# Weight pieces in one list of thirteen places, or in separate pools for raw pieces, block sums and split pieces

## The chip, the cores and the metric

One Trainium2 chip, one of its cores. The metric is the device time of the whole program in microseconds (us); lower is better. Before the change three runs gave a median of 2485.02 us (2480.92 to 2485.55).

## The reference

A two-layer decoder trunk over 256 tokens of width 2048, all in float32. Each layer adds a normed mixer and then a normed SwiGLU feed-forward network (5632 hidden columns) to its input:

```python
for layer in range(DEPTH):
    u = rms_norm(h, mix_norm_pre[layer])
    u = even_mixer(u, ...) if layer % 2 == 0 else odd_mixer(u, ...)
    h = h + rms_norm(u, mix_norm_post[layer])
    u = swiglu(rms_norm(h, ffn_norm_pre[layer]), ffn_w_gate[layer], ffn_w_up[layer], ffn_w_down[layer])
    h = h + rms_norm(u, ffn_norm_post[layer])
```

The even mixer is stick-breaking attention beside a gated delta rule, the odd one block-sparse attention beside dilated attention; each has one projection of the input ahead of it and one of the output behind it. Nearly all arithmetic is the product of 256 tokens with the weights (about 400 MB, each read once).

## The kernel before

**Pieces.** The weights are cut on the host into pieces of 128 partitions x 2 x 512 columns, 512 KB, which is 4 KB in each partition. `Builder.run` lines them up in one list of steps, 808 in all: even input projection, even output projection, feed-forward, then the same for the odd layer. Each phase runs in `run_phase`.

**A plain piece** is loaded by SP (L247) and then split for exact products in TensorE's fp32r format: ACT copies it rounded (L222, the high part), DVE subtracts that from the raw values (L223, the low part). In feed-forward phases one operation on each engine does the whole piece (128x1024), elsewhere two of 128x512. TensorE then makes 12 matmuls of 512 columns (`step`, L280 to L282: two halves of the piece, high x high, high x low, low x high, for two blocks of 128 tokens). The high and the low part lie in one tile of 8 KB per partition.

**A seven-product piece** (the last three steps of a `FastChunk`, which is every up chunk of the feed-forward network and every gate chunk but the first) uses a Strassen-like scheme: DVE forms four block sums (L266 on 512 columns, L267 and L268 on 256), the seven blocks of 256 columns are split by one ACT and one DVE operation (128x1792), and TensorE makes 21 matmuls of 256 columns (`fast_step`, L304 to L306) in the place of 24 matmuls' worth of products. Its split parts need two places of 8 KB. There are 42 such chunks, so 126 such pieces; a chunk is five plain pieces and then three seven-product pieces.

**The order of feed-forward chunks.** The 11 column groups are taken in pairs: up, gate, up and gate chunks follow each other, then four down chunks of the pair before (16 plain pieces), and so on.

**The places.** All of this lies in one list of 13 places of 8 KB, `self.wp`, handed out first in, first out, by the program that writes the instructions. A raw plain piece takes half a place (`self.half`, shared with the next one). A raw seven-product piece takes a whole one, its lower half the weights, its upper half the four sums. `load_until(n)` writes the instructions that load and split piece after piece ahead of step n. It stops at ten steps ahead, or when too few places are free:

```python
need = s.places + (not held or s.pair is not None)
if len(self.wp.free) < need + (self.spare - 1 - held if self.loaded > n else 0):
    break
```

`self.spare` is 5 in feed-forward phases: with no half open, a plain piece is taken up when 6 of the 13 places are free, a seven-product piece when 7 are. Each of the 13 places is a tile with a tag of its own, so a transfer or a split waits for the last reader of just the place that it was given.

**What sets the order on the engines.** The program above fixes the data flow and a priority; a scheduler places the instructions on the five queues by its own estimate of when each could run. All queues run in order on the chip.

Of the kernel before, what the change touches and what calls it, by code (L numbers as in the profile page):

```python
# [28 lines left out]
F32 = mybir.dt.float32  # L29
F32R = mybir.dt.float32r  # L30
# [5 lines left out]
P = 128  # L36
# [6 lines left out]
EPS = 1e-6  # L43
NEG = -1.0e30
WB = 10
WPLACES = 13
SPARE = 3
SPARE_FFN = 5
LAG_FFN = 1
DEFER = 5  # L50
LAG = 4
# [13 lines left out]
class Step:  # L65
# [3 lines left out]
    def __init__(self, src, kts, chunk, first, last, pair=None):  # L69
        self.src, self.kts, self.chunk, self.first, self.last, self.pair = src, kts, chunk, first, last, pair  # L70
        self.wh = self.wl = None
        self.ends = last
        self.places = 1 if pair is None else 2
# [73 lines left out]
class Builder:  # L147
    def __init__(self, tc, I, out, pool):
        self.tc, self.nc, self.I, self.out = tc, tc.nc, I, out
        self.const = pool("const", bufs=1)  # L150
        wpool = pool("w", bufs=1)
        self.tmp = pool("tmp", bufs=1)
        big = pool("big", bufs=1)
        psb = pool("psb", bufs=1, space=PSUM)
        dram = pool("dram", bufs=1, space=bass.MemoryType.DRAM)
        self.mem = Pool(big, "m", NTILES)
        self.wp = Pool(wpool, "w", WPLACES, (P, 2048))
        self.spare, self.lag, self.half = SPARE, LAG, None
        self.ps = Pool(psb, "p", NPS)
        self.pa = Pool(psb, "acc", PSA)  # L160
        self.cin = Pool(big, "c", 2, (P, 4, P + 3))
        self.xd = dram.tile([2 * P, D], F32, name="xd", tag="xd")
        self.nwd = dram.tile([4, D], F32, name="nwd", tag="nwd")
        self.work, self.steps, self.flags, self.loaded = [], [], set(), 0
        self.unsplit = [set(), set()]
        self.S = None
        self.x, self.y, self.yss, self.aT, self.r = ([None] * 2 for _ in range(5))
        self.mix = [{}, {}]
# [60 lines left out]
    def load_until(self, n, end=None):  # L229

        nc = self.nc
        while self.loaded < min(n + WB if end is None else end, len(self.steps)):
            s = self.steps[self.loaded]
            held = self.half is not None
            need = s.places + (not held or s.pair is not None)
            if len(self.wp.free) < need + (self.spare - 1 - held if self.loaded > n else 0):
                break
            s.w = [self.wp.pop(1) for i in range(s.places)]
            w = [a.bitcast(F32R) for a in s.w]
            if s.pair is None:  # L240
                n_ = s.src.shape[2]
                done = self.half
                self.half = done or self.wp.pop(1)
                raw = self.half[:, 1024:] if done else self.half[:, :1024]
                raw, s.wh, s.wl = (a.rearrange("p (k n) -> p k n", k=2)[:, :, :n_]
                                   for a in (raw, w[0][:, :1024], w[0][:, 1024:]))
                nc.sync.dma_start(out=raw, in_=s.src)  # L247
                if s.chunk.ffn:
                    self.split(s.wh, s.wl, raw)
                else:  # L250
                    for j in range(2):
                        self.split(s.wh[:, j], s.wl[:, j], raw[:, j])
                if done:
                    self.half = None
            else:
                done = self.wp.pop(1)
                nc.sync.dma_start(out=done[:, :1024], in_=s.src.rearrange("p k n -> p (k n)"))
                self.split_sums(done.rearrange("p (b n) -> p b n", b=8), s, *w)
            if done:
                self.wp.give(done)  # L260
            self.loaded += 1

    def split_sums(self, b, s, wh, wl):

        nc = self.nc
        nc.vector.tensor_sub(b[:, 4:6], b[:, 0:1].broadcast_to([P, 2, 256]), b[:, 1:3])  # L266
        nc.vector.tensor_sub(b[:, 6], b[:, 1], b[:, 5])  # L267
        nc.vector.tensor_sub(b[:, 7], b[:, 3], b[:, 6])  # L268
        s.wh, s.wl = (a.rearrange("p (b n) -> p b n", b=8)[:, :7] for a in (wh, wl))
        self.split(s.wh, s.wl, b[:, 1:8])  # L270

    def step(self, t, s):
        nc, ch = self.nc, s.chunk
# [63 lines left out]
    def run_phase(self, lo, hi, end):  # L337

        n0 = n1 = lo
        while n1 < hi:  # L340
            edge = n0 - lo < LAG_EDGE or hi - n0 <= LAG_EDGE - self.lag
            lag = LAG_EDGE if edge else max(self.lag, LAG_EDGE - (n0 - lo - LAG_EDGE) // 2)
            if n0 < hi and self.steps[n0].pair is not None:
                if n0 == n1:
                    self.fast_step(self.steps[n0])
                    self.wp.give(*self.steps[n1].w)
                    n0 += 1
                    n1 += 1
                    self.load_until(n1)
                    continue  # L350
                lag = 0
            if n0 < hi and n0 - n1 < lag:
                self.step(0, self.steps[n0])
                n0 += 1
                if n0 == hi:
                    end(0)
            else:
                self.step(1, self.steps[n1])
                self.wp.give(*self.steps[n1].w)
                n1 += 1  # L360
                self.load_until(n1)
        end(1)
# [134 lines left out]
    def run(self):  # L497
        nc, I = self.nc, self.I
        phases = [self.plan_even_in(), self.plan_out(0), self.plan_ffn(0),
                  self.plan_odd_in(), self.plan_out(1), self.plan_ffn(1)]  # L500
        ends = [lambda t: self.end_in(t, 0), lambda t: self.end_out(t, 0), lambda t: self.end_ffn(t, 0),
                lambda t: self.end_in(t, 1), lambda t: self.end_out(t, 1), lambda t: self.end_ffn(t, 1)]
        bounds = []
        for chunks in phases:
            lo = len(self.steps)
            for c in chunks:
                self.steps += c.steps
            bounds.append((lo, len(self.steps)))
        nc.scalar.preload_act_table_set("natural_log_exp_and_others")
        self.ident = self.ld("ident", [P, P])  # L510
        self.nw = self.ld("nw", [P, 4 * KT])
        self.zero = self.fill("zero", [P, P], 0.0)
        self.mhalf = self.fill("mhalf", [P, 8], -0.5)
        self.warm_up()
        self.aT = [[], []]
        self.x = [self.now(self.mem, 4) for t in range(2)]
        for c in range(4):
            for t in range(2):
                self.load_x(t, c, I["x"], nc.sync)
            self.load_until(0, 2 * c + 2)  # L520
        for c in range(4):
            for t in range(2):
                self.first_transposed(t, c)
        for t in range(2):
            self.prenorm_factor(t)
            self.mem.give(*self.x[t])
        self.load_until(0)
        self.load_constants()
        for i, ((lo, hi), end) in enumerate(zip(bounds, ends)):
            if i % 3 == 2:  # L530
                for j in range(PS_FFN):
                    self.ps.lend(self.pa)
                if i == 2:
                    self.mem.give(*self.lev)
                else:
                    self.mem.give(self.mask)
                self.spare, self.lag = SPARE_FFN, LAG_FFN
            self.run_phase(lo, hi, end)
            self.spare, self.lag = SPARE, LAG
            if i % 3 == 2:  # L540
                for j in range(PS_FFN):
                    self.pa.lend(self.ps)
# [798 lines left out]
```

## Time and profile before

| | |
|---|---|
| runs | 2485.02 us median of 3 |
| the profiled execution | 2482.63 us, of which the span of the program's instructions is 2480.9 us |
| TensorE matmul (PE) busy | 2395.2 us, 97% |
| DVE busy | 1752.4 us, 71% |
| ACT busy | 1222.8 us, 49% |
| DMA | 453.67 MB, mean 183 GB/s over the span |
| mean granted TensorE clock | 0.985 |

A row of the profile gives an engine, a source line and the tiles written and read. Matmuls are pipelined, so one that is shown as 0.39 us long is followed by the next after 0.23 us; a gap in the rows is shorter than the time lost. The clock of TensorE is given as a share of its full rate: 1.00 is 2.4 GHz, 0.5 is 1.2 GHz. The feed-forward network of the first layer runs from about 545 to 1300 us, that of the second from about 1710 us to the end.

### The profile page before, as it was taken

What the parts mean: (1) busy time and instruction counts of PE and PEld (TensorE: products, weight loads), DVE (VectorE), ACT (ScalarE), POOL (GpSimd) and SP (SyncE); (2) the same over time, 40 slices, a digit from 0 to 9 for tenths busy, and PEclk for the clock granted to TensorE, in tenths of its full rate; (3) what the DMA queues carried; (4) which work ended last, traced back from release to release, by engine and by line L of the source; (5) the groups of instructions that cost most, each with busy time, mean ns of one, the idle gap of its engine ahead of it and who ended that gap; (6) DMA issues with size and microseconds to landing.
All of it is one profiled execution on the core that took longest, in us unless ns stands there. A gap on an engine that the chain in (4) does not pass through costs nothing.

```text
span 2480.9 us, 32443 instructions
## 1 busy us (share of the span) xinstructions
PE 2395.2 (97%) x12235; PEld 2005.1 (81%) x12235; DVE 1752.4 (71%) x2669; ACT 1222.8 (49%) x1833; POOL 206.2 (8%) x265
## 2 busy tenths in 40 slices
PE   9999999899999999999999999999999999999998
PEld 7878877778888887888877888887878888888876
DVE  7865775577868787778776555566776868687775
ACT  6654563454545444445455544454454535444443
POOL 0330360200000000000121000101000000000011
PEclk9999999999999999999999999999999999999999
DMA  6533434454545645555575444554464645555563
GB/s 235 196 136 136 153 136 149 152 192 163 199 165 187 212 162 197 185 212 178 204 259 186 160 168 181 206 205 166 158 229 161 215 156 204 186 186 180 189 245 126
DMA packets 131133, 453.67 MB, mean 183 GB/s; under 512 B 15568, under 2 KB 20944, under 8 KB 130976
## 3 DMA queue, kind: packets, MB, share of 16 engines
q1 hardware_dynamic: 120704, 423.81, 48.5%
q0 software_dynamic: 8112, 26.52, 3.3%
q8 instruction: 96, 1.57, 0.3%
q10 hardware_dynamic: 2160, 1.27, 0.2%
q14 instruction: 61, 0.50, 0.1%
HBM read 443.11 MB, written 8.42 MB: 182 GB/s over the span
## 4 chain that ended last, share of the span: by engine, by line
PE 65%; DVE 8%; DMA 8%; ACT 3%; issue 2%; POOL 0%; SPq 0%; DVEq 0%; POOLq 0%; ACTq 0%
PE acc L280 9%; PE p L281 9%; PE p L282 9%; PE p L280 9%; PE acc L281 9%; PE acc L282 9%; DVE w L223 4%; DMA w<-in_ffn_w_gate 4%; DMA w<-in_ffn_w_up 3%; ACT w L222 2%; PE acc L305 1%; PE acc L306 1%; PE p L305 1%; PE acc L304 1%; PE p L306 1%
## 5 line engine op out<-in xcount | busy, mean ns | idle before, releaser
L223 DVE TENSOR_TENSOR w<-w,w 128x512 fp32r<-128x512 f32 (+3 forms) x1104 | 1112.7, 1040 | 482.1 <-ACT w L222 479.7
L222 ACT ACTIVATE w<-w 128x512 fp32r<-128x512 f32 (+3 forms) x1104 | 944.4, 892 | 929.0 <-DVE w L268 287.6
L280 PE MATMUL acc<-w,m 128*128 128x512 f32 (+2 forms) x1582 | 622.3, 396 | 16.3 <-ACT w L222 9.0
L281 PE MATMUL acc<-w,m 128*128 128x512 f32 (+2 forms) x1582 | 622.0, 394 | 0.0
L282 PE MATMUL acc<-w,m 128*128 128x512 f32 (+2 forms) x1582 | 621.5, 394 | 0.2 <-DVE m L226 0.2
L280 PE MATMUL p<-w,m 128*128 128x512 f32 x1146 | 454.2, 399 | 10.7 <-ACT w L222 8.7
L281 PE MATMUL p<-w,m 128*128 128x512 f32 x1146 | 455.3, 397 | 0.9 <-DVE w L223 0.8
L282 PE MATMUL p<-w,m 128*128 128x512 f32 x1146 | 454.9, 398 | 0.0
L280 PEld LDWEIGHTS acc<-w,m 128*128 128x128 f32 x1582 | 299.5, 190 | 82.5 <-ACT w L222 10.2
L282 PEld LDWEIGHTS acc<-w,m 128*128 128x128 f32 x1582 | 298.8, 189 | 66.6 <-DVE m L226 0.6
L281 PEld LDWEIGHTS acc<-w,m 128*128 128x128 f32 x1582 | 299.0, 189 | 65.6 <-DVE w L223 0.6
L280 PEld LDWEIGHTS p<-w,m 128*128 128x128 f32 x1146 | 216.0, 189 | 60.7 <-ACT w L222 10.7
L281 PEld LDWEIGHTS p<-w,m 128*128 128x128 f32 x1146 | 216.0, 188 | 51.2 <-DVE w L223 2.4
L282 PEld LDWEIGHTS p<-w,m 128*128 128x128 f32 x1146 | 216.0, 189 | 49.8 <-DVE m L223 0.2
L266 DVE TENSOR_TENSOR w<-w 128x512 f32<-128x512 f32 x126 | 86.8, 689 | 91.0 <-DMA w<-in_ffn_w_up 54.8
L305 PE MATMUL acc<-w,m 128*128 128x256 f32 x462 | 130.9, 285 | 5.3 <-DVE w L223 5.3
L304 PE MATMUL acc<-w,m 128*128 128x256 f32 x462 | 128.1, 284 | 6.8 <-ACT w L222 6.7
L306 PE MATMUL acc<-w,m 128*128 128x256 f32 x462 | 130.3, 284 | 0.0
L433 POOL DMA_DIRECT2D m<-in_ffn_norm_post x16 | 8.8, 551 | 1342.0 <-PE acc L282 663.1
L305 PE MATMUL p<-w,m 128*128 128x256 f32 x420 | 118.3, 284 | 1.3 <-DVE w L223 1.3
L306 PE MATMUL p<-w,m 128*128 128x256 f32 x420 | 117.7, 282 | 0.0
L304 PE MATMUL p<-w,m 128*128 128x256 f32 x420 | 114.4, 282 | 3.0 <-ACT w L222 3.0
(268 smaller groups left out, 2115.3 us busy)
## 6 DMA issues: line engine op xcount, KB each, us to landing
w<-in_ffn_w_gate SPq DMA_DIRECT2D x176, 512.0 KB, 4.1
w<-in_ffn_w_up SPq DMA_DIRECT2D x176, 512.0 KB, 3.8
w<-in_ffn_w_down SPq DMA_DIRECT2D x176, 512.0 KB, 4.7
w<-in_ev_w_in SPq DMA_DIRECT2D x104, 512.0 KB, 4.4
w<-in_od_w_in SPq DMA_DIRECT2D x96, 512.0 KB, 4.3
w<-in_ev_w_out SPq DMA_DIRECT2D x32, 512.0 KB, 4.6
w<-in_od_w_out SPq DMA_DIRECT2D x32, 512.0 KB, 4.5
xd<-m POOLq DMA_DIRECT2D x24, 256.0 KB, 4.1
```

What stands on the lines that cost most here:

```text
L222: self.nc.scalar.activation(h, src, AF.Copy)
L223: self.nc.vector.tensor_sub(l, src, h.bitcast(F32))
L266: nc.vector.tensor_sub(b[:, 4:6], b[:, 0:1].broadcast_to([P, 2, 256]), b[:, 1:3])
L280: nc.tensor.matmul(acc, xh, s.wh[:, j], start=(s.first and j == 0), stop=False)
L281: nc.tensor.matmul(acc, xh, s.wl[:, j], start=False, stop=False)
L282: nc.tensor.matmul(acc, xl, s.wh[:, j], start=False, stop=end)
L304: nc.tensor.matmul(acc, xh, s.wh[:, b], start=s.first and i in (0, 2), stop=True, **kw)
L305: nc.tensor.matmul(acc, xh, s.wl[:, b], start=False, stop=True, **kw)
L306: nc.tensor.matmul(acc, xl, s.wh[:, b], start=False, stop=True, **kw)
L433: self.nc.gpsimd.dma_start(out=w, in_=src.broadcast_to([P, 512]))
```

## The change

The one list becomes three pools. Four raw pieces of 4 KB, two sets of block sums of 4 KB, and ten split pieces of 8 KB; together 104 KB per partition, as before. The tiles of a pool share one tag, so any free buffer of the pool serves. `load_until` now stops when the steps from n on would need more than ten split pieces, in all phases alike; the numbers that kept places spare are gone. Nothing is given back by hand: a buffer is free when its last reader is done. The block sums go to a tile of their own, and so a seven-product piece is split by two operations on each engine: three blocks from the raw piece (128x768) and four from the sums (128x1024).

```diff
 WB = 10
-WPLACES = 13
-SPARE = 3
-SPARE_FFN = 5
+RAW = 4
...
-        wpool = pool("w", bufs=1)
+        self.wpool = pool("w", bufs=WB)
+        self.rpool = pool("raw", bufs=RAW)
+        self.spool = pool("sums", bufs=2)
...
-            held = self.half is not None
-            need = s.places + (not held or s.pair is not None)
-            if len(self.wp.free) < need + (self.spare - 1 - held if self.loaded > n else 0):
+            if sum(a.places for a in self.steps[n:self.loaded + 1]) > WB:
                 break
-            s.w = [self.wp.pop(1) for i in range(s.places)]
-            w = [a.bitcast(F32R) for a in s.w]
+            raw = self.rpool.tile([P, 1024], F32, name="raw", tag="raw")
+            w = [self.wpool.tile([P, 2048], F32R, name="w", tag="w") for i in range(s.places)]
...
-        nc.vector.tensor_sub(b[:, 4:6], b[:, 0:1].broadcast_to([P, 2, 256]), b[:, 1:3])
-        nc.vector.tensor_sub(b[:, 6], b[:, 1], b[:, 5])
-        nc.vector.tensor_sub(b[:, 7], b[:, 3], b[:, 6])
         s.wh, s.wl = (a.rearrange("p (b n) -> p b n", b=8)[:, :7] for a in (wh, wl))
-        self.split(s.wh, s.wl, b[:, 1:8])
+        t = self.spool.tile([P, 1024], F32, name="sums", tag="sums").rearrange("p (b n) -> p b n", b=4)
+        nc.vector.tensor_sub(t[:, 0:2], b[:, 0:1].broadcast_to([P, 2, 256]), b[:, 1:3])
+        nc.vector.tensor_sub(t[:, 2], b[:, 1], t[:, 1])
+        nc.vector.tensor_sub(t[:, 3], b[:, 3], t[:, 2])
+        self.split(s.wh[:, :3], s.wl[:, :3], b[:, 1:4])
+        self.split(s.wh[:, 3:], s.wl[:, 3:], t)
```

**SP's queue, first layer's feed-forward network, where a gate chunk's seven-product pieces end and a down chunk begins.** L257 is the load of a seven-product piece, L247 that of a plain one; in brackets are the engines and DMA queues whose counters the load waits for. Before:

```order
L257 DMA w8_9003<-in_ffn_w_gate 128x1024 [waits DVE_49,PE_49]
L257 DMA w7_9026<-in_ffn_w_gate 128x1024 [waits DMAHW5_49,PE_49]
L257 DMA w8_9077<-in_ffn_w_gate 128x1024 [waits DMAHW6_49,DMAHW4_49,DVE_49]
L247 DMA w1_9171<-in_ffn_w_down 128x1024 [waits DMAHW7_49,PE_49]
L247 DMA w1_9171<-in_ffn_w_down 128x1024 [waits DMAHW0_49]
```

And with the change, where the same loads stand at L248 and L241:

```order
L248 DMA raw_9254<-in_ffn_w_gate 128x1024 [waits DMAHW0_49,DVE_49]
L248 DMA raw_9298<-in_ffn_w_gate 128x1024 [waits DMAHW1_49,DVE_49]
L248 DMA raw_9324<-in_ffn_w_gate 128x1024 [waits DMAHW2_49,DVE_49]
L241 DMA raw_9348<-in_ffn_w_down 128x1024 [waits DMAHW3_49,DVE_49]
L241 DMA raw_9383<-in_ffn_w_down 128x1024 [waits DMAHW4_49,DVE_49]
```

The wait for PE is gone from the loads: what remains is DVE, which frees a raw piece by its split.

**DVE's queue, two seven-product pieces of the first layer's feed-forward network.** The tiles w2 and w1 hold raw weights and sums, w8 and w7 the low parts. Before:

```order
L266 TENSOR_TENSOR w2_7343<-w2_7343 128x512
L267 TENSOR_TENSOR w2_7343<-w2_7343 128x256
L268 TENSOR_TENSOR w2_7343<-w2_7343 128x256
L223 TENSOR_TENSOR w8_7342<-w2_7343,w10_7341 128x1792
L725 TENSOR_TENSOR m30_6288<-m30_6288,p4_7298 128x512
L266 TENSOR_TENSOR w1_7380<-w1_7380 128x512
L725 TENSOR_TENSOR m43_6296<-m43_6296,p3_7305 128x512
L267 TENSOR_TENSOR w1_7380<-w1_7380 128x256
L268 TENSOR_TENSOR w1_7380<-w1_7380 128x256
L223 TENSOR_TENSOR w7_7379<-w1_7380,w3_7378 128x1792
```

With the change (sums at L257 to L259, low parts at L222), for the first two such pieces of a gate chunk:

```order
L258 TENSOR_TENSOR sums_7722<-raw_7718,sums_7722 128x256
L259 TENSOR_TENSOR sums_7722<-raw_7718,sums_7722 128x256
L222 TENSOR_TENSOR w_7665<-raw_7664,w_7665 128x1024
L257 TENSOR_TENSOR sums_7766<-raw_7762 128x512
L222 TENSOR_TENSOR w_7693<-raw_7692,w_7693 128x1024
L258 TENSOR_TENSOR sums_7766<-raw_7762,sums_7766 128x256
L222 TENSOR_TENSOR w_7720<-raw_7718,w_7719 128x768
L259 TENSOR_TENSOR sums_7766<-raw_7762,sums_7766 128x256
L222 TENSOR_TENSOR w_7720<-sums_7722,w_7719 128x1024
L302 TENSOR_TENSOR m8_7752<-m28_7751,acc1_7669 128x256
L222 TENSOR_TENSOR w_7764<-raw_7762,w_7763 128x768
L222 TENSOR_TENSOR w_7764<-sums_7766,w_7763 128x1024
```

The sums of the second piece now stand ahead of the first one's split, and each split is two operations.

**PE's queue, start of the first feed-forward network.** L384 (L373 with the change) are the transposes of the second block's normed input, which wait for the chain of norms on DVE, ACT and GpSimd. Before:

```order
L280 MATMUL acc_5153<-w_5183,m_4863 128x512
L281 MATMUL acc_5153<-w_5183,m_4863 128x512
L282 MATMUL acc_5153<-w_5183,m_4864 128x512
L384 MATMUL p_5008<-ident,m_4438 128x128 x4
L384 MATMUL p_5018<-ident,m_4586 128x128 x4
L384 MATMUL p_5028<-ident,m_4747 128x128 x4
```

With the change:

```order
L271 MATMUL acc_5245<-w,m_4936 128x512
L272 MATMUL acc_5245<-w,m_4936 128x512
L273 MATMUL acc_5245<-w,m_4937 128x512
L373 MATMUL p_5095<-ident,m_4512 128x128 x4
L373 MATMUL p_5105<-ident,m_4664 128x128 x4
L373 MATMUL p_5115<-ident,m_4829 128x128 x4
```

The transposes come earlier: between the first block's batch and this one stood 70 single matmuls and now stand 58.

## Rows read from the trace of the kernel before

**Rows 1.** The page, ahead of part 1 and in it: engine, busy us (share) xinstructions.
```profile
span 2480.9 us, 32443 instructions
...
PE 2395.2 (97%) x12235; PEld 2005.1 (81%) x12235; DVE 1752.4 (71%) x2669; ACT 1222.8 (49%) x1833; POOL 206.2 (8%) x265
```

**Rows 2.** Busy time of each engine in the two feed-forward stretches.
```profile
560.00:1240.00 680.00, 666.35 (x3545) 565.99 (x3544) 517.17 (x636) 323.56 (x315) 7.03 (x14) 0.99 0.54 187
1765.00:2440.00 675.00, 657.22 (x3460) 556.02 (x3459) 511.30 (x620) 317.95 (x312) 8.58 (x16) 0.99 0.56 193
```

**Rows 3.** PE's waits, first feed-forward stretch: us, times, longest.
```profile
PE acc L280 <- ACT w L222: 6.5, 4, 2.5
...
PE acc L304 <- ACT w L222: 1.8, 3, 0.8
```

**Rows 4.** PE's waits, second feed-forward stretch.
```profile
PE acc L305 <- DVE w L223: 5.3, 4, 1.3
...
PE p L304 <- ACT w L222: 0.3, 1, 0.3
```

**Rows 5.** Busy time in 10 us round two slow-clock stretches, clock behind POOL.
```profile
634.00:644.00 10.00, 7.21 (x47) 6.82 (x48) 10.00 (x7) 5.42 (x5) 0.00 (x0) 0.83 0.17 59
...
2402.00:2412.00 10.00, 7.68 (x27) 5.36 (x26) 6.36 (x10) 3.45 (x4) 1.47 (x3) 0.83 0.99 367
```

**Rows 6.** Timeline, PE, plain pieces: start us, us, engine, line, operation.
```profile
1289.98 0.39 PE L280 MATMUL acc<-w,m 128*128 128x512 f32 x1
...
1300.24 0.40 PE L282 MATMUL acc<-w,m 128*128 128x512 f32 x1
```

**Rows 7.** Timeline, PE, seven-product pieces.
```profile
1000.10 0.28 PE L304 MATMUL acc<-w,m 128*128 128x256 f32 x1
...
1001.12 0.28 PE L304 MATMUL p<-w,m 128*128 128x256 f32 x1
```

**Rows 8.** Groups by line and shape, DVE and ACT (busy us, mean ns, idle before).
```profile
L223 DVE TENSOR_TENSOR w<-w,w 128x1024 fp32r<-128x1024 f32 x386 | 462.9, 1221 | 170.9 <-ACT w L222 169.8
...
L223 DVE TENSOR_TENSOR w<-w,w 128x512 fp32r<-128x512 f32 x560 | 386.8, 730 | 235.8 <-ACT w L222 234.6
...
L222 ACT ACTIVATE w<-w 128x1024 fp32r<-128x1024 f32 x386 | 400.6, 1057 | 330.7 <-DMA w<-in_ffn_w_down 123.8 <-DVE w L223 66.3 <-DMA w<-in_ffn_w_up 65.1
...
L223 DVE TENSOR_TENSOR w<-w,w 128x1792 fp32r<-128x1792 f32 x126 | 254.3, 2022 | 72.2 <-ACT w L222 72.2
...
L222 ACT ACTIVATE w<-w 128x1792 fp32r<-128x1792 f32 x126 | 212.9, 1699 | 297.5 <-DVE w L268 287.6 <-issue 4.1 <-PE acc L282 3.7
...
L266 DVE TENSOR_TENSOR w<-w 128x512 f32<-128x512 f32 x126 | 86.8, 689 | 91.0 <-DMA w<-in_ffn_w_up 54.8 <-DMA w<-in_ffn_w_gate 34.9 <-PE p L306 0.7
...
L267 DVE TENSOR_TENSOR w<-w 128x256 f32<-128x256 f32 x126 | 52.4, 421 | 1.7
```

**Rows 9.** The page, part 6: DMA issues, KB each, median us to landing.
```profile
w<-in_ffn_w_gate SPq DMA_DIRECT2D x176, 512.0 KB, 4.1
```

**Rows 10.** Waits of SP's DMA queue.
```profile
SPq L247 <- PE acc L282: 691.1, 131, 30.8
```

**Rows 11.** Timeline, SP, three seven-product pieces of one gate chunk.
```profile
912.06 11.17 SPq L257 DMA_DIRECT2D w<-in_ffn_w_gate  x3
```

**Rows 12.** Timeline, DVE, the third of them.
```profile
926.39 0.69 DVE L266 TENSOR_TENSOR w<-w 128x512 f32<-128x512 f32 x1 [1.65 <-DMA w<-in_ffn_w_gate]
```

**Rows 13.** Timeline, PE, the same piece.
```profile
932.08 0.39 PE L304 MATMUL acc<-w,m 128*128 128x256 f32 x1 [0.79 <-ACT w L222]
```

**Rows 14.** PE's waits, start of the second feed-forward network.
```profile
PE acc L384 <- DVE m L479: 4.5, 1, 4.5
```

**Rows 15.** Busy time of each engine in 10 us with dense transfers.
```profile
951.00:961.00 10.00, 10.00 (x45) 8.05 (x44) 7.74 (x8) 5.30 (x6) 0.00 (x0) 1.00 0.94 337
```

**Rows 16.** Chain that ended last, in order of time: a long transfer.
```profile
536.94 8.36 DMA w<-in_ffn_w_gate
```

More of the change, by code (lines that the diff above doesn't have):

```diff
@@ L156, in __init__ @@
         self.mem = Pool(big, "m", NTILES)
-        self.wp = Pool(wpool, "w", WPLACES, (P, 2048))
-        self.spare, self.lag, self.half = SPARE, LAG, None
+        self.lag = LAG
         self.ps = Pool(psb, "p", NPS)
@@ L233, in load_until @@
             s = self.steps[self.loaded]
-            held = self.half is not None
-            need = s.places + (not held or s.pair is not None)
-            if len(self.wp.free) < need + (self.spare - 1 - held if self.loaded > n else 0):
+            if sum(a.places for a in self.steps[n:self.loaded + 1]) > WB:
                 break
-            s.w = [self.wp.pop(1) for i in range(s.places)]
-            w = [a.bitcast(F32R) for a in s.w]
+            raw = self.rpool.tile([P, 1024], F32, name="raw", tag="raw")
+            w = [self.wpool.tile([P, 2048], F32R, name="w", tag="w") for i in range(s.places)]
             if s.pair is None:
                 n_ = s.src.shape[2]
-                done = self.half
-                self.half = done or self.wp.pop(1)
-                raw = self.half[:, 1024:] if done else self.half[:, :1024]
                 raw, s.wh, s.wl = (a.rearrange("p (k n) -> p k n", k=2)[:, :, :n_]
@@ L252, in load_until @@
                         self.split(s.wh[:, j], s.wl[:, j], raw[:, j])
-                if done:
-                    self.half = None
-            else:
[L256 to L260, printed above, removed]
+            else:
+                nc.sync.dma_start(out=raw, in_=s.src.rearrange("p k n -> p (k n)"))
+                self.split_sums(raw.rearrange("p (b n) -> p b n", b=4), s, *w)
             self.loaded += 1
@@ L345, in run_phase @@
                     self.fast_step(self.steps[n0])
-                    self.wp.give(*self.steps[n1].w)
                     n0 += 1
@@ L358, in run_phase @@
                 self.step(1, self.steps[n1])
-                self.wp.give(*self.steps[n1].w)
                 n1 += 1
@@ L536, in run @@
                     self.mem.give(self.mask)
-                self.spare, self.lag = SPARE_FFN, LAG_FFN
+                self.lag = LAG_FFN
             self.run_phase(lo, hi, end)
-            self.spare, self.lag = SPARE, LAG
+            self.lag = LAG
             if i % 3 == 2:
```

## The prediction

> **What bounds the kernel now.** I read the page first: PE is busy for 2395.2 of 2480.9 us, 97% [rows 1]. DVE has 71% and ACT 49%, so over the whole span neither is the bound; what a better supply of weights can give back is only time in which PE stands still or runs slowly. I then cut the span into stretches and looked at where PE loses time, and for what.
>
> In the first feed-forward stretch PE is busy for 666.35 of 680 us, in the second for 657.22 of 675 [rows 2]. That is 13.65 + 17.78 = 31.4 us of gaps. PE's waits there name nothing but split weights: four rows with 11 waits in the first, six rows with 15 in the second, all of them on ACT at L222 or DVE at L223, the two halves of a split [rows 3, 4]. In the mixers and projections PE also loses time, but its waits there name the attention chains and the norms, not weights, and I take those as unchanged at first.
>
> Why are the weights late? SP's queue tells: its loads wait 691 us in total for one group of PE's matmuls [rows 10], since a transfer needs a place that PE has finished with. In a feed-forward chunk there is a second tie. The three seven-product pieces of one gate chunk are issued over 11.17 us [rows 11]. The third of them gets the place of the first one's raw weights, so its transfer starts only when DVE has split that one, at about 923 us. DVE then waits for it to land and starts its sums at 926.39 [rows 12], ACT's rounding follows, and PE, which has run out, starts at 932.08 [rows 13]. Transfer, sums and split stand in one row and PE is at its end. Such stalls return through both networks.
>
> **What these stalls cost: the sum.** Three terms.
>
> (a) The gaps themselves: 31.4 us [rows 2].
>
> (b) What the rows hide of them. A plain matmul is shown as 0.39 us, but 44 of them start in 1300.24 - 1289.98 = 10.26 us, so the next one is due after 0.233 [rows 6]; a seven-product matmul is shown as 0.28 and is due after 1.02 / 9 = 0.113 [rows 7]. Each gap is thus short by about 0.16 us; 26 waits x 0.16 = 4.2 us.
>
> (c) The clock. After eight of these stalls the granted clock shows 0.83 over ten us, that is 1.2 GHz for 3.4 us of them; two of the eight rows are shown [rows 5]. 10 x 0.17 = 1.7 us lost each, 13.6 us in all. Before each of them PE had stood still.
>
> Together 31.4 + 4.2 + 13.6 = 49.2 us in the two feed-forward networks.
>
> **The change, part by part.**
>
> *Loads no longer wait for PE.* With the change a load waits for DVE alone, as SP's queue shows: piece k for the split of piece k - 4. The split waits for PE to finish what lies ten split places back. For the third seven-product piece of a chunk these ten places are its own two, four of its two neighbours and four plain pieces. So its split may start 4 x 12 x 0.233 + 2 x 21 x 0.113 = 11.2 + 4.7 = 15.9 us of PE work ahead of its use, and its transfer and sums earlier still. Before, such a piece is taken up with 7 of 13 places free, so it, its neighbours and two plain pieces fill eight: 5.6 + 4.7 = 10.3 us. In those it had to fit transfer 4.1 [rows 9], sums 0.69 + 2 x 0.42, ACT 1.70 and DVE 2.02 [rows 8] = 9.4 us, with 0.9 to spare for every delay in DVE's queue. Now it must fit ACT's two operations and DVE's last, about 1.06 + 0.85 + 1.22 = 3.1 us, in 15.9: nearly 13 us of room. A plain down piece behind the three has ten places too: itself, six and three plain, 3 x 2.8 + 3 x 2.4 = 15.6 us, against 2.3 us of split. I therefore let all 49.2 us go. Cover gone would show as the same waits at L304 and L280.
>
> *Two operations instead of one.* On ACT 768 columns more cost 1699 - 1057 = 642 ns, so 0.836 ns a column and a fixed 201 ns an operation [rows 8]: 126 x 0.2 = 25 us. On DVE the fixed part is 153 ns by the step from 1024 to 1792 columns and 239 by that from 512 to 1024 [rows 8]: 126 x 0.15 to 0.24 = 19 to 30 us, I take 25. All of it lies beside PE: in the feed-forward stretches DVE is busy for 517 of 680 us and ACT for 324 [rows 2], and 12 us more in each still leaves DVE at 78%. Price on the path: 0. Without that cover it would be the first rival.
>
> *The last few plain pieces, the mixers.* The ten steps of lead stay; transfers start earlier, splits at about the same step. Price 0, between -5 and +5 us, since the scheduler lays the attention chains' instructions a little differently.
>
> *The starts of the phases.* At the start of the first feed-forward network the second block's transposes now come 12 matmuls earlier on PE, so 12 x 0.233 = 2.8 us less work covers the norms they wait for. The same wait cost 4.5 us at the start of the second network [rows 14]; at the other two starts the batch also moves forward, by 8 matmuls and by 24. From below the change may give back up to 3 us of waits for weights there, from above it costs up to (12 + 8 + 24) x 0.233 = 10.3. I take +2 us, near the lower end, because only the first of the three moves into a wait that the trace shows.
>
> *SP.* More of its loads wait for two or three counters, but it only issues; with 4 raw pieces in hand that is off the path. At the program's start the last loads of x stand behind raw pieces five and six, which wait for the first two splits; those come earlier than the loads do today. Price 0.
>
> Sum: 2482.63 - 49.2 + 2 = 2435.4 us for the profiled execution. The median of the runs lies 2.4 us above that execution, so I forecast 2438 us.
>
> **The rivals.**
>
> *DVE becomes the bound in gate and up chunks.* A chunk costs PE 5 x 12 x 0.233 + 3 x 21 x 0.113 = 21.1 us. DVE needs 5 x 1.22 + 3 x (2.02 + 1.53) = 16.8 us for its splits, now 17.3, and about 3 more for closing the chunk (of the 517 us in the first stretch, 20 chunks take 336 and 88 down pieces 107, which leaves 74, some 3.5 a chunk with what belongs to the down chunks) [rows 2, 8]. 20.6 of 21.1 us leaves almost nothing for DVE's own waits on ACT, and four such chunks follow each other. If DVE waits another 0.85 to 1.06 us in each piece it falls back by 4 x 7 = 28 us in a group, more than the 16 of lead, and stalls come back. Against: where lead is full DVE need not keep up, and the down chunks (16 pieces, 45 us of PE, 20 of DVE) refill it each time. I price it at half the stalls left: 2485 - 25 + 2 = 2462 us. The Trainium skill (Perfetto Trace Analysis, Optimizing Scalar/DVE Operations) says that grouping into larger operations helps throughput when such an engine is saturated; by that rule cutting 1792 columns in two is wrong here just where DVE is full, and this rival is what it would give. The trace has DVE at 76% over the stretch, so by the rows it isn't saturated. Chance 0.12.
>
> *Four raw pieces are too few: slower.* Each raw buffer is held from the start of its transfer until DVE has split it. With H us for landing and for waiting in the queues of ACT and DVE, a plain piece holds it for H + 2.3 and a seven-product piece for H + 3.3 (sums 1.53, then about 0.85 and 0.95 for the three raw blocks) [rows 8]; a chunk holds 8 H + 21.4 us, and four buffers give 4 x 21.1 = 84.4 us in the time that PE needs. Above H = 7.9 us the loads, not PE, set the pace of the chunks. Landing alone is 4.1 now [rows 9], one of 8.36 shows in the chain [rows 16]. At 8.36 and 1 us in queues a chunk takes 96.3 / 4 = 24.1 us, 3.0 more than PE, 42 x 3.0 = 126 us: about 2485 - 49 + 126 = 2562 us. Against: the engines of the DMA moved 337 GB/s in a dense stretch [rows 15], at which one piece takes 1.6 us, and the mean need is 187 [rows 2]. Chance 0.03.
>
> *The change doesn't do what it says.* The scheduler sets the order by its own estimate; if splits stand late in the queues, or the mixers lose what the feed-forward networks gain, the time stays at 2480 to 2490 us. For it: PE's order did change in the mixers. Against: in the feed-forward networks the split of a piece hangs on PE work more than ten us before its use, wherever I looked. Chance 0.05.
>
> **How the numbers follow.** My forecast, the stalls gone, has 0.80: 2422 to 2450 us by the bounds of the phase starts (-3 to +10), the mixers (+-5) and (b) and (c), which may be a few us too small. Up to the first rival's 2462 the range holds 0.8 and more: 2422 to 2462 us. A measurement can tell about 0.2%, 5 us, from no change. Faster by more than that: 0.80 + 0.12 = 0.92, of which I take off 0.01 for a mixer that loses more than I allow, so 0.91. Within it: 0.05. Slower: 0.03 and that 0.01, 0.04.
>
> **What would show it.** Right: in both feed-forward stretches PE's waits on L221 and L222 (the split lines with the change) nearly gone, PE busy over 99% there, no slow-clock stretch between 560 and 1200 us; ACT's and DVE's busy time up by about 25 us each; SP's waits on DVE instead of PE; the span near 2435 us. Wrong: the same stall once a column pair with DVE over 95% in front of it (first rival); landings near 8 us and ACT waiting for transfers (second); longer gaps at the starts of phases or in the attention chains than the 10 us I allow.

## The result, and the profile after

With the change the kernel takes 2428.32 us (median of 4 runs, 2424.63 to 2431.17), against 2484.78 us for the kernel before on the same chip (4 runs, 2480.92 to 2485.55): a ratio of 0.9775, 95% interval 0.9756 to 0.9794. The profiled execution is the slowest of the four, 2431.17 us.

The page of the changed kernel, ahead of part 1 and in it, and two of its DMA issues (KB each, median us to landing); they answer to [rows 1, 9]:

```profile
span 2429.4 us, 33249 instructions
...
PE 2377.0 (98%) x12235; PEld 1999.0 (82%) x12235; DVE 1755.2 (72%) x2795; ACT 1249.3 (51%) x1959; POOL 213.7 (9%) x265
...
raw<-in_ffn_w_gate SPq DMA_DIRECT2D x176, 512.0 KB, 3.8
raw<-in_ffn_w_up SPq DMA_DIRECT2D x176, 512.0 KB, 4.2
```

The span is 51.5 us shorter. ACT has 26.5 us more to do, DVE only 2.8 us more, although both have 126 operations more.

The two feed-forward stretches, where the second lies 50 us earlier than before (busy us of PE, its weight loads, DVE, ACT and POOL; then clock, DMA share, GB/s). They answer to [rows 2]:

```profile
560.00:1240.00 680.00, 680.00 (x3656) 578.61 (x3655) 537.81 (x716) 348.30 (x395) 6.45 (x12) 1.00 0.61 198
1715.00:2390.00 675.00, 674.86 (x3611) 575.07 (x3610) 530.14 (x698) 340.96 (x384) 8.59 (x16) 1.00 0.61 200
```

31.4 us of gaps have become 0.14, and the clock shows 1.00 over both stretches. PE has no row of waits left in either; over the whole span only one row names split weights. These are PE's longest waits with the change, and the one on weights:

```profile
PE p L1155 <- POOL m L1140: 8.5, 2, 5.8
PE p L373 <- DVE m L468: 5.8, 1, 5.8
PE acc L373 <- DVE m L468: 4.8, 1, 4.8
PE p L373 <- DVE m L459: 4.7, 1, 4.7
...
PE p L272 <- DVE w L222: 0.2, 1, 0.2
```

L373 are the transposes at the starts of the phases, L1155 belongs to the even mixer. SP's loads wait for DVE now, where PE was the first to be named [rows 10]:

```profile
SPq L241 <- DVE w L222: 1284.6, 508, 27.9
SPq L248 <- DVE w L222: 297.0, 116, 17.3
```

And the groups of the split, DVE and ACT, with the idle time before them, as in [rows 8]:

```profile
L222 DVE TENSOR_TENSOR w<-raw,w 128x1024 fp32r<-128x1024 f32 x386 | 469.5, 1221 | 183.2 <-ACT w L221 181.9
L221 ACT ACTIVATE w<-raw 128x1024 fp32r<-128x1024 f32 x386 | 407.8, 1060 | 510.8 <-PE p L273 248.6 <-PE acc L273 114.3 <-DMA raw<-in_ffn_w_down 50.4
...
L222 DVE TENSOR_TENSOR w<-sums,w 128x1024 fp32r<-128x1024 f32 x126 | 153.4, 1217 | 1.0 <-ACT w L221 1.0
L221 ACT ACTIVATE w<-sums 128x1024 fp32r<-128x1024 f32 x126 | 132.7, 1054 | 34.1 <-DVE sums L259 33.1
L222 DVE TENSOR_TENSOR w<-raw,w 128x768 fp32r<-128x768 f32 x126 | 120.0, 953 | 52.9 <-PE p L273 34.9 <-PE acc L273 17.7 <-ACT w L221 0.3
```

ACT used to stand before the seven-product split for 287.6 us, waiting for the last sum (L268) [rows 8]; before the operation on the sums it now waits 33.1 us. And before plain pieces it waits for PE, 362.9 us: raw weights have landed and wait for a split place. That is what plenty looks like.

**One measure for all kernels.** To see what each kernel loses in a network I take the time between the starts of the first and the last seven-product matmul in PE's timeline: for the first network 1235.5 - 589.3 = 646.2 us before and 1206.2 - 588.1 = 618.1 with the change. Between these marks lie the same seven-product matmuls everywhere, but not always the same plain ones: in the old list the scheduler puts some plain matmuls of the next chunk between the last seven-product ones. The two networks before, then with the change, in the columns of [rows 2]:

```profile
589.30:1235.55 646.25, 632.60 (x3386) 538.51 (x3384) 496.38 (x598) 313.25 (x301) 3.06 (x6) 0.99 0.54 189
1753.03:2400.10 647.07, 631.61 (x3385) 537.50 (x3384) 489.54 (x594) 305.25 (x297) 4.13 (x8) 0.99 0.54 188
```
```profile
588.15:1206.19 618.04, 618.04 (x3371) 528.28 (x3370) 490.28 (x653) 315.80 (x356) 3.28 (x7) 1.00 0.61 195
1729.40:2349.02 619.62, 619.62 (x3372) 531.02 (x3370) 491.24 (x653) 315.74 (x357) 4.36 (x9) 1.00 0.60 195
```

Before, 28 more matmuls of 512 columns start between the marks. At the 0.233 us of [rows 6] that is 6.5 us of work, not of loss. The table gives this count, and "networks" is the time between the marks less 0.233 us for each matmul more; "rest" is what is left of the profiled span (mixers, starts and ends of phases).

| kernel | run, us | between the marks, us | matmuls more | networks, us | rest, us |
|---|---|---|---|---|---|
| before | 2484.78 | 646.2 + 647.1 = 1293.3 | 28 | 1286.8 | 1194.1 |
| the change | 2428.32 | 618.1 + 619.6 = 1237.7 | 0 | 1237.7 | 1191.7 |
| old list, more lead | 2673.84 | 686.5 + 776.0 = 1462.5 | 23 | 1457.1 | 1216.4 |
| old list, two operations on ACT and DVE | 2446.53 | 633.7 + 623.9 = 1257.6 | 24 | 1252.0 | 1192.5 |
| old list, two on DVE only | 2467.89 | 645.7 + 632.9 = 1278.6 | 16 | 1274.9 | 1187.8 |
| old list, two on ACT only | 2434.76 | 620.8 + 623.1 = 1243.9 | 2 | 1243.4 | 1188.4 |
| old list, two on ACT, both behind sums | 2450.62 | 626.4 + 635.3 = 1261.7 | 14 | 1258.4 | 1187.6 |
| pools, 3 buffers for raw and sums, one operation | 2494.72 | 643.8 + 642.8 = 1286.6 | 0 | 1286.6 | 1209.8 |
| the same, two operations | 2467.06 | 626.8 + 630.0 = 1256.8 | 0 | 1256.8 | 1211.2 |
| pools, 3 raw pieces, own sums, two operations | 2441.15 | 618.5 + 620.8 = 1239.3 | 0 | 1239.3 | 1201.9 |
| pools, 4 buffers for raw and sums, one operation, 8 split pieces | 2436.22 | 618.3 + 619.6 = 1237.9 | 0 | 1237.9 | 1198.5 |
| the change with 8 split pieces | 2434.31 | 618.0 + 619.6 = 1237.6 | 0 | 1237.6 | 1195.3 |
| the change, more DVE operations | 2427.75 | 618.3 + 619.5 = 1237.8 | 0 | 1237.8 | 1190.2 |
| the change, nine pieces ahead | 2432.40 | 619.0 + 618.9 = 1237.9 | 0 | 1237.9 | 1193.2 |

Each run's time is the median on its own chip; where it counts, the ratio to the kernel before on that chip stands with the experiment. The other columns come from one profiled execution of each kernel. Five kernels meet at 1237.6 to 1237.9: there PE has no gap between the marks, and the networks lose nothing to weights. The change gave back 49.1 us in the networks, and the rest is 2.4 us shorter.

### The profile page after: what moved, and what is told of

Same layout as the page of the kernel before. It is cut to its first block, busy times and chain, and to the rows that moved or that the text cites. A ratio compares the mean times of both kernels' runs of the same rounds, so it can differ in the third digit from the quotient of the medians.

```text
span 2429.4 us, 33249 instructions
## 1 busy us (share of the span) xinstructions
PE 2377.0 (98%) x12235; PEld 1999.0 (82%) x12235; DVE 1755.2 (72%) x2795; ACT 1249.3 (51%) x1959; POOL 213.7 (9%) x265
## 4 chain that ended last, share of the span: by engine, by line
PE 77%; DVE 1%; DMA 1%; issue 1%; ACT 0%; POOL 0%; DVEq 0%; POOLq 0%; ACTq 0%
PE p L271 11%; PE p L273 11%; PE p L272 11%; PE acc L273 10%; PE acc L271 10%; PE acc L272 10%; PE acc L295 2%; PE acc L296 2%; PE acc L297 2%; PE p L295 2%; PE p L296 2%; PE p L297 2%; PE p L216 1%; DMA raw<-in_ffn_w_gate 1%; DVE w L222 1%
## 5 line engine op out<-in xcount | busy, mean ns | idle before, releaser
L222 DVE TENSOR_TENSOR w<-raw,w 128x512 fp32r<-128x512 f32 (+4 forms) x1104 | 986.3, 915 | 469.9 <-ACT w L221 413.7
L221 ACT ACTIVATE w<-raw 128x512 fp32r<-128x512 f32 (+4 forms) x1104 | 844.2, 795 | 863.5 <-PE p L273 328.7
L271 PE MATMUL acc<-w,m 128*128 128x512 f32 (+2 forms) x1582 | 624.0, 395 | 3.0 <-ACT m L224 2.6
L271 PE MATMUL p<-w,m 128*128 128x512 f32 x1146 | 455.2, 397 | 3.1 <-ACT m L221 3.1
L271 PEld LDWEIGHTS acc<-w,m 128*128 128x128 f32 x1582 | 299.7, 189 | 68.6 <-ACT m L224 3.1
L271 PEld LDWEIGHTS p<-w,m 128*128 128x128 f32 x1146 | 216.0, 188 | 52.1 <-ACT m L221 3.5
L222 DVE TENSOR_TENSOR w<-sums,w 128x1024 fp32r<-128x1024 f32 x126 | 153.4, 1217 | 1.0 <-ACT w L221 1.0
L221 ACT ACTIVATE w<-sums 128x1024 fp32r<-128x1024 f32 x126 | 132.7, 1054 | 34.1 <-DVE sums L259 33.1
L257 DVE TENSOR_TENSOR sums<-raw 128x512 f32<-128x512 f32 x126 | 86.8, 689 | 52.8 <-DMA raw<-in_ffn_w_gate 29.9
L295 PE MATMUL p<-w,m 128*128 128x256 f32 x420 | 117.4, 280 | 0.0
```

Source lines behind the costliest of these rows:

```text
L221: self.nc.scalar.activation(h, src, AF.Copy)
L222: self.nc.vector.tensor_sub(l, src, h.bitcast(F32))
L257: nc.vector.tensor_sub(t[:, 0:2], b[:, 0:1].broadcast_to([P, 2, 256]), b[:, 1:3])
L271: nc.tensor.matmul(acc, xh, s.wh[:, j], start=(s.first and j == 0), stop=False)
L295: nc.tensor.matmul(acc, xh, s.wh[:, b], start=s.first and i in (0, 2), stop=True, **kw)
```

## The experiments

The theory after the result was the prediction's: loads that need not wait for PE bring weights in time. It has three rivals: more lead alone, the two operations, and the split places.

**More lead in the old list.**

```diff
-SPARE_FFN = 5
+SPARE_FFN = 3
```

> The kernel before with its spare places in the feed-forward networks cut from 5 to 3, so that up to ten places instead of eight hold split pieces; raw and split pieces still share the list. Theory (the loads are tied to PE and to each other by the shared list): fewer places are free, each is handed out sooner after its last use, transfers start later; no gain, 0 to 60 us slower than before. Rival (what counted is only how many split pieces lie ahead): most of the 56 us gained, near 2430 us.

2673.84 us, ratio 1.0762 (1.0731 to 1.0794): far worse. As I read it, in one list whatever is taken up earlier takes a place from what comes next, raw or split. SP's waits of the kernel before, and of this one:

```profile
SPq L257 <- DVE w L223: 125.1, 30, 10.0
```
```profile
SPq L257 <- DVE w L223: 343.7, 56, 14.3
```

Loads of seven-product pieces wait for splits almost three times as long. The rival falls, and the size that I gave for the loss was far too small.

**Fewer split places.**

```diff
-WB = 10
+WB = 8
```

> The changed kernel with eight split pieces instead of ten, in all phases. Theory: with loads free of PE, eight places leave 10.3 us for a split of 3.1 us, so PE's waits for weights stay away in the feed-forward networks; 2428 us within 8, what is lost lies at the starts of phases. Rival (the number of split pieces ahead is what counted, it was eight before): most of the 49 us of stalls come back, 2465 to 2485 us.

2434.31 us, ratio 0.9791 (0.977 to 0.9813). The networks take 1237.6 us as with ten; the rest takes 3.6 us more. So the 15.9 us of room between split and use, on which the prediction laid weight, are not needed: with two plain pieces fewer it is 15.9 - 5.6 = 10.3 us, and nothing comes late.

**One operation, three larger buffers.** Raw piece and sums share a buffer of 8 KB, the seven blocks are split by one operation.

```diff
-RAW = 4
+RAW = 3
...
-        self.spool = pool("sums", bufs=2)
...
-            raw = self.rpool.tile([P, 1024], F32, name="raw", tag="raw")
+            both = self.rpool.tile([P, 2048], F32, name="raw", tag="raw")
+            raw = both[:, :1024]
...
+        self.split(s.wh, s.wl, b[:, 1:8])
```

> The changed kernel with three raw buffers of 8 KB in place of four raw of 4 KB and two sums of 4 KB, the sums again in the upper half of the raw buffer and a seven-product piece split by one operation on each engine. Theory (separate pools do it, the two operations are only their price): 2428 us within 6, ACT's and DVE's busy time 25 us less each. Rival (shorter operations let PE's piece be ready sooner, which is part of the gain): 10 to 30 us slower than the changed kernel, with PE's waits on split lines back in the feed-forward networks.

2494.72 us, ratio 1.004 (1.0025 to 1.0055): the whole gain is gone, and my theory with it. None of SP's waits names PE here, as with the change, and still the networks lose 48.9 us, as much as before: loads that need not wait for PE are not enough. The edit had two parts, one operation and three buffers, and the next runs took them apart. The trace shows the loss under a new name. PE's waits between 560 and 1200 us:

```profile
PE p L215 <- DVE m L682: 15.6, 12, 3.3
```

L215 transposes the product of gate and up, which DVE forms at L682. One such place, in the timelines of ACT, DVE and PE:

```profile
911.14 1.06 ACT L220 ACTIVATE w<-raw 128x1024 fp32r<-128x1024 f32 x1 [4.50 <-DMA raw<-in_ffn_w_gate]
```
```profile
912.24 3.72 DVE L221 TENSOR_TENSOR w<-raw,w 128x1024 fp32r<-128x1024 f32 x3 [3.86 <-ACT w L220]
...
916.99 0.69 DVE L256 TENSOR_TENSOR raw<-raw 128x512 f32<-128x512 f32 x1 [0.70 <-DMA raw<-in_ffn_w_gate]
...
919.47 0.69 DVE L256 TENSOR_TENSOR raw<-raw 128x512 f32<-128x512 f32 x1 [0.79 <-DMA raw<-in_ffn_w_gate]
...
922.28 0.68 DVE L682 TENSOR_TENSOR m<-m,m 128x512 f32<-128x512 f32 x1
922.88 0.68 DVE L306 TENSOR_TENSOR m<-m,acc 128x512 f32<-128x512 f32 x1
```
```profile
923.02 0.66 PE L215 MATMUL p<-ident,m 128*128 128x128 f32 x4 [3.33 <-DVE m L682]
```

First ACT waits 4.50 us for a transfer and DVE 3.86 us for ACT; then DVE stands twice more for a transfer, since the sums are next in its queue, and the product behind them is late. Weights that come late need not show as a wait for weights.

**The same buffers with two operations; four such buffers with one.** Both edits are against the run before.

```diff
-        self.split(s.wh, s.wl, b[:, 1:8])
+        self.split(s.wh[:, :3], s.wl[:, :3], b[:, 1:4])
+        self.split(s.wh[:, 3:], s.wl[:, 3:], b[:, 4:8])
```

> Three raw buffers of 8 KB that hold weights and sums together, as in the run with one operation that took 2494.7 us, but now two operations. Theory 'operation': one long operation holds the chain up, the number of buffers matters little; so the gain comes back: 2430 to 2440 us. Rival 'buffers': a raw buffer is held until the whole split is done, and three are too few. A chunk then holds them for 8 H + 5 x 2.28 + 3 x 3.81 = 8 H + 22.8 us instead of 8 H + 27.1, of 3 x 21.1 = 63.3 us, so the two operations move the threshold only from H = 4.5 to 5.1 us, and landing alone is 4: 2465 to 2495 us.

```diff
-WB = 10
-RAW = 3
+WB = 8
+RAW = 4
```

> The one operation of 1792 columns again, with four raw buffers of 8 KB instead of three; eight split pieces instead of ten pay for the memory, which alone gave 2434.3 us. Theory 'operation': as long as the split is one operation the stalls stay, 2480 to 2500 us. Rival 'buffers': four buffers give 84.4 us for 8 H + 27.1, H may reach 7.2 us, nothing stalls: 2432 to 2442 us.

2467.06 us, ratio 0.9938 (0.9923 to 0.9953), and 2436.22 us, ratio 0.9812 (0.9797 to 0.9827). The rival "buffers" holds in both. With a fourth buffer one long operation loses nothing in the networks:

```profile
560.00:1200.00 640.00, 640.00 (x3441) 544.70 (x3440) 501.67 (x613) 319.37 (x310) 1.13 (x2) 1.00 0.58 191
```

In the pools, then, the two operations are not needed to remove the stalls. Where buffers are short they do help: with three, two operations take 29.8 of the 48.9 us away.

**Three raw pieces in the changed kernel.**

```diff
-RAW = 4
+RAW = 3
```

> The change with three raw pieces of 4 KB instead of four. Theory: the prediction's second rival holds with its numbers, a chunk holds raw buffers for 8 H + 21.3 us of 3 x 21.1 = 63.3, threshold H = 5.25 us, near what landing (4) and a wait in the queues make; with shared buffers (threshold 5.1) it was 2467. So 2445 to 2465 us. Rival: with the sums in a pool of their own and two operations, three are enough, 2426 to 2434 us.

2441.15 us, ratio 0.9824 (0.9799 to 0.9848): slower than the change by some 12 us, between the two ranges, and most of it in the rest, 10.2 us. In the networks, to which the formula speaks, three are nearly enough. By the formula of the prediction's second rival the loads fall behind above H = 4.5 us (three shared buffers, one operation), 5.1 (the same, two operations), 5.25 (this run) and over 7 with four buffers. The networks lose 48.9, 19.1, 1.6 and 0.2 us against the 1237.7 of the change, in the same order. By the formula H, landing and queues together, is then about 5 us; landing alone has medians of 3.5 to 4.2 for gate and up pieces in the kernels with pools. This is an estimate; H itself was not measured.

**Two operations in the old list.**

```diff
-        self.split(s.wh, s.wl, b[:, 1:8])
+        self.split(s.wh[:, :3], s.wl[:, :3], b[:, 1:4])
+        self.split(s.wh[:, 3:], s.wl[:, 3:], b[:, 4:8])
```

> The kernel before with a seven-product piece split by two operations on each engine (three blocks, then four), nothing else. Theory: the shared list still ties the loads, 0 to 20 us slower than before by 25 us more work on each engine in a chain that is late already. Rival (shorter operations are part of the gain): 10 us or more faster than before.

2446.53 us, ratio 0.9838 (0.9812 to 0.9865). The rival holds: the operations that I had priced at nothing give 34.8 of the 49.1 us in the networks without any pool. Which engine's?

```diff
-        self.split(s.wh, s.wl, b[:, 1:8])
+        nc.scalar.activation(s.wh, b[:, 1:8], AF.Copy)
+        nc.vector.tensor_sub(s.wl[:, :3], b[:, 1:4], s.wh[:, :3].bitcast(F32))
+        nc.vector.tensor_sub(s.wl[:, 3:], b[:, 4:8], s.wh[:, 3:].bitcast(F32))
```

> The old list, ACT with one operation of 1792 columns, DVE with two. Theory 'chain': from the transfer's end to the last low part the old kernel needs 1.53 (sums) + 1.70 + 2.02 = 5.25 us, with two operations on both engines 1.53 + 1.06 + 1.22 = 3.81, because ACT rounds the three raw blocks beside the sums; here it is 1.53 + 1.70 + 0.95 + 1.22 = 5.40, no shorter, and only the first product's low part comes 1.1 us earlier. So no gain: 2475 to 2490 us. Rival 'short operations': shorter operations on DVE let other work in between, whatever the chain: most of the 37 us that two operations on both engines gave, 2445 to 2460 us.

```diff
-        self.split(s.wh, s.wl, b[:, 1:8])
+        nc.scalar.activation(s.wh[:, :3], b[:, 1:4], AF.Copy)
+        nc.scalar.activation(s.wh[:, 3:], b[:, 4:8], AF.Copy)
+        nc.vector.tensor_sub(s.wl, b[:, 1:8], s.wh.bitcast(F32))
```

> The old list, ACT with two operations, DVE with one. Theory 'chain': 1.53 + 1.06 + 2.02 = 4.61 us, 0.64 of the 1.44 us that two operations on both engines save; so 0.64 / 1.44 of their 37 us, 16 us faster: 2460 to 2475 us. Rival 'short operations on DVE': no gain, 2478 to 2490 us.

On DVE only 2467.89 us, ratio 0.9943 (0.9925 to 0.996); on ACT only 2434.76, ratio 0.9806 (0.9792 to 0.9821). It is ACT more than DVE: ACT's second operation alone removes 43.4 of the 49.1 us in the networks, DVE's alone 11.9. Both theories had the sizes wrong: "chain" gave ACT 16 us and DVE none, "short operations" the gain to DVE. ACT's waits in the whole span, ahead of and behind the cut (L222 split the whole piece before; L271 splits the four blocks of sums):

```profile
ACT w L222 <- DVE w L268: 287.6, 88, 8.2
```
```profile
ACT w L271 <- DVE w L268: 92.8, 70, 4.6
```

The wait has moved rather than gone: ahead of the first operation ACT now stands 207.9 us for transfers (130.7 for up pieces, 77.2 for gate pieces), and it rounds the raw blocks while DVE forms the sums. And the loads wait for PE as before. The row on which the prediction built, 691.1 us [rows 10], is the same in this kernel, where the networks lose 5.7 us (L284 is L282 before):

```profile
SPq L247 <- PE acc L284: 691.3, 130, 30.6
```

**Two operations on ACT, both behind the sums.** Odd and even blocks in the place of raw and summed ones.

```diff
-        nc.scalar.activation(s.wh[:, :3], b[:, 1:4], AF.Copy)
-        nc.scalar.activation(s.wh[:, 3:], b[:, 4:8], AF.Copy)
+        nc.scalar.activation(s.wh[:, 1::2], b[:, 2:8:2], AF.Copy)
+        nc.scalar.activation(s.wh[:, 0::2], b[:, 1:8:2], AF.Copy)
```

> The old list, ACT with two operations of 768 and 1024 columns, DVE with one, as in the run that took 2434.8 us, but cut by odd and even blocks: the first operation now needs the second and third sums too, so neither can begin before L267. The durations are the same. Theory 'sums': what counted was that ACT could round the three raw blocks without the sums, so that less stands behind the last sum; from landing to ACT's end it is 1.11 + 0.85 + 1.06 = 3.02 us here, 2.59 there, 3.23 with one operation: a third of the 48 us, 2460 to 2480. Rival 'short operations on ACT': two shorter operations do it wherever they stand: 2432 to 2442 us.

2450.62 us, ratio 0.9863 (0.984 to 0.9885), between the two. In the networks 28.4 of the 43.4 us remain. ACT waits for the sums nearly as long as with one operation (250.1 + 16.9 against 287.6 us), but is done with them sooner:

```profile
L271 ACT ACTIVATE w<-w 128x1024 fp32r<-128x1024 f32 x126 | 131.5, 1048 | 17.5 <-DVE w L268 16.9
L270 ACT ACTIVATE w<-w 128x768 fp32r<-128x768 f32 x126 | 105.7, 843 | 257.3 <-DVE w L267 250.1 <-PE acc L284 6.2
```

Behind the last sum there is 1.05 us of ACT's work where there was 1.70. That, not the time at which ACT begins, fits the larger part of the gain; the rest may belong to the operation that needs no sums. Neither is shown: the scheduler orders every one of these kernels differently (28 plain matmuls more between the marks before, 2 with two operations on ACT, 14 here), and these runs do not tell how much of the gain is the order.

**More DVE operations in the changed kernel.** A raised cost: the low part of every plain feed-forward piece is formed by two operations.

```diff
-                    self.split(s.wh, s.wl, raw)
+                    nc.scalar.activation(s.wh, raw, AF.Copy)
+                    for j in range(2):
+                        nc.vector.tensor_sub(s.wl[:, j], raw[:, j], s.wh[:, j].bitcast(F32))
```

> The change, and besides every plain feed-forward piece gets two DVE operations of 512 columns instead of one of 1024. Two take 2 x 0.724 us instead of 1.221, so 0.23 us more for each of 386 pieces, 88 us more of DVE, about 1.1 us a gate or up chunk: DVE goes from 87% of a group of four such chunks to some 93%. Theory 'hidden': where PE no longer waits for weights, DVE's fixed cost of an operation lies beside PE even now: 2426 to 2438 us. Rival, the prediction's first: DVE is full in the groups, each group then falls behind by up to 4 x 1.1 us, 10 groups: 2445 to 2475 us.

2427.75 us, ratio 0.9753 (0.9729 to 0.9777): no difference from the change. The cost was smaller than meant; DVE's total in the page, one group of four chunks, and the new operations:

```profile
PE 2372.4 (98%) x12235; PEld 1994.3 (82%) x12235; DVE 1781.3 (73%) x3181; ACT 1251.0 (52%) x1959; POOL 214.8 (9%) x265
```
```profile
847.00:923.00 76.00, 76.00 (x465) 66.98 (x465) 68.50 (x113) 42.26 (x49) 0.00 (x0) 1.00 0.61 195
```
```profile
L245 DVE TENSOR_TENSOR w<-raw,w 128x512 fp32r<-128x512 f32 x772 | 496.3, 687 | 156.9 <-ACT w L243 154.6
```

386 more operations make DVE 26.1 us busier, not 88. In the group it is at 90%, where the change has 87% (66.31 of the same 76 us), and PE does not stand. The first rival, DVE full, is out at that load; a higher one was not tried.

**A try for a better version.**

```diff
-LAG_EDGE = 8
+LAG_EDGE = 9
```

> A try for a better version: the change with the first block of tokens nine instead of eight pieces ahead at the edges of a phase, to cover the norms that the second block's transposes wait for (15.3 us in three waits). One piece more is 6 x 0.233 = 1.4 us at each of three starts: 2424 us if that is all. Rival: nine pieces ahead and the tenth in use leave no split place for the next piece, and the starts get longer: 2432 to 2445 us.

2432.40 us, ratio 0.9788 (0.9763 to 0.9813): no gain over the change that these runs can tell. The time is the rival's, but its reason does not show: the waits at the transposes fell, from 15.2 to 12.6 us, and only one wait of 0.6 us names a split weight. What the starts lose was not to be had that way; none of these kernels is measurably better than the change.

## Why the prediction was right, and where it was not

**The time.** 2438 us was forecast, 2428.32 came, inside the range and 10 us below the forecast. About half of that is the step from the profiled execution to the median: the median lay 2.9 us below it, where I added 2.4. The other 4 us are mostly one term of the sum, (b).

**The gaps and the clock.** The three terms had the right things in them: no gap, no row of waits, no slow clock is left. Between the marks the networks gave back 49.1 us. The rows there show 13.65 + 15.46 = 29.1 us of gaps, and seven of the eight slow-clock stretches lie there, 7 x 1.7 = 11.9 us. That leaves 8.1 us for what the rows hide of 24 waits, 0.34 us each, where (b) took 0.16: (a) and (c) were right, (b) was half of what it should be. Two waits and the eighth slow stretch, some 4 us by the prediction's own prices, lie behind the last mark, in the rest.

**The starts.** With that stall gone the rest should have been some 4 us shorter, less the 2 us that I took for the starts; it was 2.4 us shorter. The price is about right, from two sides: PE's waits at the transposes grew from 7.3 to 15.2 us, as bounded, while those on weights outside the marks fell from 6.0 to 0.2 and all others from 31.6 to 25.2.

**The reason** stands in part. With four raw buffers in a pool of their own the stalls are gone even with one long operation, as forecast. Three steps of the argument fell, and the time does not show it, because the change holds two remedies for the same stalls:

- That weights are late because loads wait for PE. With three shared buffers no load waits for PE, and the networks lose 48.9 us; with two operations on ACT in the old list the loads wait for PE as long as before (691.3 us), and the networks lose 5.7. In the pools what counts is how long a buffer is held and how many there are. Of the two ties that the prediction named, the second, the place that a piece gets only when DVE has split another, fits this, but no run loosens it by itself in the old list.
- "Price on the path: 0" for the two operations. Inside the pools with four buffers this is right (one operation 2436.2, two 2434.3, both with eight split pieces). But I had worked out myself that a piece's chain takes 9.4 us of 10.3, with 0.9 to spare, and then looked at the two operations only as work for busy engines. They also shorten that chain: behind the last sum by 0.64 us on ACT, and by my reading twice in a row, since the third piece waits for the split of the first [rows 11, 12]. The kernel with the old list and two operations on ACT only reaches 2434.8. So the change removes one stall by two means, each nearly enough; their gains do not add.
- The room of 15.9 us between split and use. Eight split pieces do as well as ten in the networks.

**The rivals.** DVE as the bound did not show up, neither by the change nor with 386 operations more. Its price of 20.6 us of DVE in the 21.1 us of a chunk added up the lengths of rows, and rows of DVE overlap (last section): with the change DVE is busy for 87% of a group. The Trainium skill (Perfetto Trace Analysis, Optimizing Scalar/DVE Operations) has, beside the rule on grouping that the prediction weighed, the opposite one for engines that are not saturated but hold others up: shorter instructions may complete work sooner. The runs on ACT agree with that one: 43.4 us in the networks, with ACT at 49% before. The second rival, too few raw pieces, had the right mechanism: three are too few, four are enough, and the formula put the runs in the right order.

**What was to be seen.** PE's waits on split weights gone: yes. PE over 99% busy: yes, 99.99%. No slow clock from 560 to 1200 us: yes. SP waiting for DVE: yes. ACT 25 us busier: yes, 26.5. DVE 25 us busier: no, 2.8. The span near 2435: 2429.4.

## What to carry to other kernels

Price a split instruction twice: as load on its engine, and as the stretch of the dependent chain that it shortens; where the chain had less than a microsecond to spare, the second was what counted here. Ahead of a deeper prefetch, work out how long each buffer is held from the start of its transfer to the end of its last reader, and compare buffers times the consumer's pace with that sum: here three against four raw buffers decided 12 to 58 us, two split places nothing in the networks. A large sum of waits in a queue is not yet a cause: the 691 us of loads waiting for PE stood unchanged in a kernel without the stalls. And look for late weights behind other names too, since a queue that runs in order passes the delay on to whatever stands next.

## What the runs showed of the hardware

A DVE operation costs less than its row says when others stand next to it. One of 512 columns has a row of 687 ns in the run with more DVE operations, one of 1024 a row of 1221 ns with the change; two for one should cost 153 ns more, and cost 26.1 us / 386 = 68 ns of busy time. The rows overlap, as in the timeline above, where L682 at 922.28 us has 0.68 us and DVE's next operation starts at 922.88. This is part of why the change added 25.7 us to the sum of DVE's split groups (742.9 against 717.2 us) and only 2.8 to its busy time. The 126 operations more on DVE alone, in the old list, made it 7.7 us busier (1760.1 against 1752.4), 61 ns each; what else became less with the change is not shown. The Trainium skill (Perfetto Trace Analysis, Optimizing Scalar/DVE Operations) gives about 60 ns of fixed busy time for such an operation and says that the shown latency is about twice that, half of it beside the next one; the 68 ns agree.

In the old list two operations on DVE helped where ACT had one (11.9 us in the networks) and hurt where ACT had two (8.6 us more than on ACT only). The cause stays open.
